# Rows of a multiple of 128 bytes for the moving operands, weights an odd multiple of 64 bytes from them

## The chip, the cores and the metric

The kernel runs on one core of a Trainium2 chip. The metric is the time of one execution on the device, in microseconds (us); lower is better. Three runs of the kernel before give a median of 2256.5 us (2256.18 to 2257.68).

## What is computed

One decoder layer on 1040 tokens (16 learned meta tokens ahead of 1024) of width 1024, in float32: a half-step feed-forward network, a mixing block with two groups of heads, a second feed-forward network, and a last norm. Cut to what matters:

```python
n = rms_norm(h, ffn1_norm)
h = h + 0.5 * ((silu(n @ w_gate) * (n @ w_up)) @ w_down)      # D_FF = 2816
n = rms_norm(h, mix_norm)
proj = n @ w_in                                               # 3 * 512 + 1696 columns
sb_out = stick_breaking_attention(q, k, v)                    # 8 heads of 64
rw_out = rwkv7_time_mix(proj[..., 1536:], ...)                # 8 heads of 64
h = h + concatenate([sb_out, rw_out]) @ w_out
n = rms_norm(h, ffn2_norm)
h = h + 0.5 * ((silu(n @ w_gate2) * (n @ w_up2)) @ w_down2)
return rms_norm(h, final_norm)[:, 16:]
```

The products with w_gate, w_up, w_down, w_in and w_out are the dense products of the title.

## The kernel before, in words

Activations are kept transposed: 128 of the 1024 features on the partitions, tokens along the row. The tokens are worked in two groups, A of 528 (16 + 512) and B of 512. A dense product takes a weight tile of 128 x 128 as the stationary operand and up to 512 tokens of an activation tile as the moving one, and sums eight such steps (or as many as the part of w_down has) in a PSUM bank.

To keep float32's precision with a faster type, every operand is split into a high and a low part of type float32r, and each step is three matmuls (mm3, line 680): high weights by high activations, high by low, low by high. ScalarE (ACT) makes the high part by a copy, VectorE (DVE) or GpSimd (POOL) the low part by a subtraction (split, line 498). Weights come from DRAM into the ring wr of two raw tiles, are split into the rings wh and wl of two tiles each (wsplit, line 526), and are used once or twice.

The moving operands are these tiles. `n` (ntiles, line 854): four tiles of 4 rows, high and low, each row NA = 528 floats. `n2B`, the same for group B of the second network, rows of 512. `ah` and `al` (act_tiles, line 947): the outcome of silu(gate) * up, one row of NA floats, in rings of four. A row is read in chunks: 512 columns at once, or 256 and 272 (256 and 256) where the network begins or ends.

Two stages work in another way. For a part of ffn1's group A and of ffn2's group B, pairs of gate or up tiles are multiplied by a scheme of Strassen's kind with seven products in place of eight ("quads": class Fast, line 466; pair, 577; sums, 1109; quad, 1143). `sums` makes four combinations of activations, the tiles t1 to t4 (4 rows of w = 264 or 256 floats); `pair` makes five combinations of weights, split into the rings qh and ql of seven tiles each; `cc` is a ring of seven tiles in which outcomes are added up. A weight tile there has rows of `qrow` = 128 + w % 128 floats, that is 136 where w is 264, and the offset of rows grows alike on both sides.

The order of the work is made when the program is built: Clock and Task (lines 168 to 460) run the stages as coroutines against costs of each instruction, and give a ring's next buffer out when its last reader is done. A coroutine says what it needs (`need`, `room`), with the ring's length beside it. The engines then follow the order written, with semaphores. TensorE works its queue in order; the waits that it meets are those on DVE, ACT or a ring of PSUM banks.

Tiles of a pool lie one behind the other, in steps of 32 bytes, and pools one behind the other; so a tile's size sets the place of all tiles behind it. Tiles that matter for places: `sl` (a gate's or up's outcome, 512 floats, two buffers), `nacc`, `nsq` and `ny` (272 floats) of the norms, `ones` (128 used floats of 152), and `f` of the attention.

The root of the norm (norm_root, line 819) is a row of reciprocal roots; norm_end (line 833) puts it into a tile `ny` of a ring of one, scales h by it and splits the outcome into `n`.

Of the kernel before, what the change touches and what calls it, by code (L numbers as in the profile page):

```python
# [7 lines left out]
F32 = mybir.dt.float32  # L8
# [8 lines left out]
P = 128  # L17
# [22 lines left out]
        dict(raw=1, qs=4, kh=4, vs=2, sg=8, f=2, at=4, z=2, t=2, o=1)]  # L40
WOUT = ((0, 1, 2, 3, 4, 5, 6, 7, 2, 3, 4, 5), (0, 1, 2, 3, 4, 5, 6, 7))
QF = dict(ffn1=6, ffn2=4)
QROW = P + 8
AHEAD = 0.1
IDLE = 0.45
BACKLOG = 3.0
# [419 lines left out]
class Fast:  # L466
# [2 lines left out]

    def __init__(self, pools, w):  # L470
        self.p, self.tp, self.q = pools
        self.w, self.nq, self.nc, self.ns, self.k = w, 7, 7, 4, 0
        self.qrow = P + w % P
        self.t = {i: [self.tp.tile([P, 4, w], F32R, name="t%d%s" % (i, c)) for c in "hl"] for i in (1, 2, 3, 4)}


class Ker:
# [40 lines left out]
    def wraw(self, src, nk, nm, ring=None):  # L518
# [4 lines left out]
        self.clock.ahead = False  # L523
        return raw

    def wsplit(self, raw, nk, nm, pool):
        self.clock.ahead = True
        self.nsplit = getattr(self, "nsplit", 0) + 1
        hi = pool.tile([P, nk, nm], F32R, tag="wh", bufs=2, name="whi")
        lo = pool.tile([P, nk, nm], F32R, tag="wl", bufs=2, name="wlo")  # L530

        self.split(hi, lo, raw, self.nc.gpsimd if self.nsplit < 3 else None)
        self.clock.ahead = False
        return hi, lo
# [42 lines left out]
    def pair(self, raws, out):  # L577


        nc, p = self.nc, self.fast.q  # L580
        nb, qrow = self.fast.nq, self.fast.qrow
        a1, a2 = raws
        lo4, hi4 = slice(0, 4), slice(4, 8)

        def part(src=None):

            for tag in ("qh", "ql"):
                yield self.need(bank=(p, tag, nb))
            if src:
                yield self.need(bank=(p, "qs", 3))  # L590
            self.clock.ahead = True
            t = [p.tile([P, 4 * QROW], F32R, tag=tag, bufs=nb, name=tag) for tag in ("qh", "ql")]
            t = [x[:, 0:4 * qrow].rearrange("p (k m) -> p k m", m=qrow)[:, :, 0:P] for x in t]
            self.hold(t)
            if src:
                x, y, op, eng = src
                raw = p.tile([P, 4 * P + 16], F32, tag="qs", bufs=3, name="qs")[:, 0:4 * P].rearrange("p (k m) -> p k m", m=P)
                self.hold((raw,))
                eng.tensor_tensor(out=raw, in0=x, in1=y, op=op)
                self.clock.ahead = False  # L600
                return t, raw
            return t

        def halves(t, raw):
            self.clock.ahead = True
            self.split(t[0], t[1], raw)
            self.clock.ahead = False
            self.drop((raw,))
            out.append((t, t))
        for tag in ("wh", "wl"):  # L610
            yield self.need(bank=(self.wp, tag, 2))
        self.clock.ahead = True
        w = [self.wp.tile([P, KT, P], F32R, tag="w" + c, bufs=2, name=n) for c, n in (("h", "whi"), ("l", "wlo"))]
        self.hold(w)
        self.clock.ahead = False
        s1 = yield from part((a2[:, lo4], a2[:, hi4], ALU.add, nc.gpsimd))
        self.clock.ahead = True
        self.split(w[0], w[1], a1)
        out.append(([w[0][:, lo4], w[1][:, lo4]], ()))
        out.append(([w[0][:, hi4], w[1][:, hi4]], w))  # L620
        self.clock.ahead = False
        s2 = yield from part((s1[1], a1[:, lo4], ALU.subtract, nc.vector))
        halves(*s1)
        a22 = yield from part()
        self.split(a22[0], a22[1], a2[:, hi4])
        self.clock.ahead = False
        s4 = yield from part((a1[:, hi4], s2[1], ALU.subtract, nc.vector))
        halves(*s2)
        out.append((a22, a22))
        s3 = yield from part((a1[:, lo4], a2[:, lo4], ALU.subtract, nc.gpsimd))  # L630
        halves(*s4)
        halves(*s3)
# [71 lines left out]
    def consts(self, cp):  # L704
        nc = self.nc
        self.ident = cp.tile([P, P], F32, name="ident")
        make_identity(self.tc.nc, self.ident)
        self.ones = cp.tile([P, P + 24], F32, name="ones")[:, 0:P]
        nc.gpsimd.memset(self.ones, 1.0)

    def consts2(self, cp, xp, psp):
# [121 lines left out]
    def norm_end(self, s, h, cols, gain, n, bank, now=True):  # L833

        nc, tp = self.nc, self.fp
        w = cols.stop - cols.start
        ys = []

        def new():
            ys.append(tp.tile([P, 272], F32, tag="ny", bufs=1, name="ny"))  # L840
            self.hold(ys)
            return ys[0][:, :w]
        yield from self.norm_root(s, w, new, bank, ("ny", 1))
        y = ys[0][:, :w]
        for k in range(KT):
            yield from self.room(tp, ("sl", 2) if k % 2 else ("nsq", 4))
            with self.urgent() if now else nullcontext():
                f = tp.tile([P, 512], F32, tag="sl", bufs=2, name="nf")[:, :w] if k % 2 else tp.tile([P, 272], F32, tag="nsq", bufs=4, name="nf")[:, :w]
                nc.vector.scalar_tensor_tensor(f, h[:, k, cols], self.v(gain, k), y, ALU.mult, ALU.mult)
                self.split(n[0][k][:, cols], n[1][k][:, cols], f, nc.gpsimd if k % 2 else None)  # L850
        self.drop(ys)
        yield self.need(*[x for k in range(KT) for x in (n[0][k][:, cols], n[1][k][:, cols])])

    def ntiles(self):

        half = [[self.hp.tile([P, 4, NA], F32R, tag="n%s%d" % (c, q), name="n%s%d" % (c, q)) for q in range(2)] for c in "hl"]
        return [[half[c][k // 4][:, k % 4, :] for k in range(KT)] for c in range(2)] + half

    def block(self, xts, m, xp, bank, out, hot=None):
# [37 lines left out]
    def ffn(self, nm, h, n, chunks, edge, bank, first=None, hook=None, wx=False, poll=None, resid=None, done=None, wy=False, fast=False, once=False):  # L897
# [32 lines left out]
        def gate(w, c0, c1):  # L930
            pg = yield from mm(*w, "pg", c0, c1)
            with self.urgent():
                sl = tp.tile([P, 512], F32, tag="sl", bufs=2, name="sl")[:, :c1 - c0]
                nc.scalar.activation(sl, pg, AF.Silu if fast else AF.Sigmoid)
                if not fast:

                    nc.vector.tensor_tensor(out=sl, in0=pg, in1=sl, op=ALU.mult)
            self.hold((sl,))
            return sl

        def up(w, sl, act, c0, c1, last):
            pu = yield from mm(*w, "pu", c0, c1)
            with self.urgent():
                nc.vector.tensor_tensor(out=sl, in0=pu, in1=sl, op=ALU.mult)
                self.split(act[0][:, c0:c1], act[1][:, c0:c1], sl, None if last else nc.gpsimd)
        gu = lambda ap, f, keep=False: self.wget(ap[:, :, f * P:f * P + P], KT, P, keep)
        act_tiles = lambda c=None: [c.q.tile([P, 2 * c.w], F32R, tag="q" + t, bufs=2, name=t) if c else
                                    tp.tile([P, NA], F32R, tag=t, bufs=4, name=t) for t in ("ah", "al")]

        def gates(f):  # L950
            if poll:
# [902 lines left out]
    def attn_z(self, pr, g, bufs, ops, out):  # L1854
# [6 lines left out]
        for i in (2 * pr, 2 * pr + 1):  # L1861
# [18 lines left out]
            for sg in sgs:  # L1880
                nc.gpsimd.affine_select(out=sg[:, S - P:S], in_=sg[:, S - P:S], pattern=[[-1, P]],
                                        compare_op=ALU.is_gt, fill=0.0, base=0, channel_multiplier=1)
                yield from self.room(ap, ("f", bufs["f"]))
                f = ap.tile([P, n], F32, tag="f", bufs=bufs["f"], name="f")
                nc.scalar.activation(f[:, :S], sg[:, :S], AF.Copy, scale=-1.0, bias=1.0)
                V.tensor_tensor_scan(f[:, S - 1::-1], f[:, S - 1::-1], f[:, S - 1::-1], 1.0, ALU.mult, ALU.bypass)
                nc.gpsimd.tensor_tensor(out=sg[:, 0:S - 1], in0=sg[:, 0:S - 1], in1=f[:, 1:S], op=ALU.mult)
# [646 lines left out]
```

## Time and profile before

| | |
|---|---|
| median of 3 runs | 2256.5 us |
| the profiled execution | 2258.75 us |
| its span (first to last instruction) | 2257.0 us |
| mean granted clock of TensorE | 0.997 |
| TensorE (PE), matmuls | 2227.9 us busy, 16409 instructions |
| weight loads (PEld) | 1972.8 us |
| VectorE (DVE) | 1550.8 us |
| ScalarE (ACT) | 1097.6 us |
| GpSimd (POOL) | 561.7 us |

Busy times of engines overlap. A matmul that overlaps the next is counted once in the busy time, while its "mean ns of one" is its own length from start to modelled end, so that for matmuls in a row the spacing from start to start is shorter than that length. Every operation is recorded by one helper, so all lines are L105 and groups are told apart by tiles: `pg<-nh,whi` is a matmul into the PSUM tile pg with nh moving and whi as weights. pg and pu are the products with w_gate and w_up, pd those with w_down and w_in, pwo that with w_out, po the attention's with v. In the chain of waits, neighbours on one engine with the same output are merged into one piece with its length and count.

### The profile page before, as it was taken

Reading aid. Unit: us, or ns where it says so; the run is one execution under the profiler, and the core shown is the slowest. Engines: PE = TensorE matmul, PEld = TensorE weight load, DVE = VectorE, ACT = ScalarE, POOL = GpSimd, SP = SyncE. Lnnn points to the kernel's source line nnn. Section 1 sums busy time; section 2 is a strip of 40 time slices with the busy share of each in tenths; the row PEclk is TensorE's granted clock in tenths of the full one; section 3 lists DMA queues with packets and bytes.
Section 4 is the critical chain, followed back from the end, with each engine's and each line's share of the span. In section 5 each row is a group of like instructions: output and inputs, shape, how many; then the busy total and the mean of one; then the engine's idle time right before and its main releaser. Section 6 shows DMA issues by size and latency. Waiting matters only on the chain.

```text
span 2257.0 us, 41723 instructions
## 1 busy us (share of the span) xinstructions
PE 2227.9 (99%) x16409; PEld 1972.8 (87%) x16409; DVE 1550.8 (69%) x2633; ACT 1097.6 (49%) x2176; POOL 561.7 (25%) x722
## 2 busy tenths in 40 slices
PE   9999999999999999999999999999999999999998
PEld 8999999999878888778878987887878899899998
DVE  5887776575666655566576887556777656897774
ACT  5444444544444534555435564445656436455444
POOL 1221111013142231442012324314443101221110
PEclk9999999999999999999999999999999999999999
DMA  5543232545633232332556534333222433333332
GB/s 167 175 119 103 81 108 78 164 129 137 204 104 102 71 102 88 108 92 71 153 146 189 167 101 117 86 93 118 82 79 61 131 117 121 113 103 104 112 88 81
DMA packets 408731, 257.62 MB, mean 114 GB/s; under 512 B 45005, under 2 KB 392357, under 8 KB 408534
## 3 DMA queue, kind: packets, MB, share of 16 engines
q1 hardware_dynamic: 408534, 254.95, 39.0%
q8 instruction: 129, 2.11, 0.4%
q14 instruction: 68, 0.56, 0.1%
HBM read 220.90 MB, written 33.99 MB: 113 GB/s over the span
## 4 chain that ended last, share of the span: by engine, by line
PE 92%; DVE 4%; ACT 1%; DMA 1%; issue 1%; POOL 0%; SPq 0%; DVEq 0%; ACTq 0%; POOLq 0%
PE pd L105 35%; PE pu L105 21%; PE pg L105 20%; PE pwo L105 4%; PE px L105 3%; PE po L105 2%; PE pz L105 2%; PE pat L105 2%; DVE wlo L105 1%; PE pG L105 1%; DVE tt L105 0%; PE psw L105 0%; ACT whi L105 0%; PE pp L105 0%; PE pss L105 0%
## 5 line engine op out<-in xcount | busy, mean ns | idle before, releaser
L105 ACT ACTIVATE whi<-wraw 128x1024 fp32r<-128x1024 f32 x314 | 330.5, 1053 | 339.0 <-PE pd L105 209.7
L105 DVE TENSOR_TENSOR wlo<-wraw,whi 128x1024 fp32r<-128x1024 f32 (+1 forms) x312 | 402.7, 1291 | 98.4 <-ACT whi L105 92.2
L105 PE MATMUL pd<-ah,whi 128*128 128x512 f32 (+2 forms) x944 | 326.0, 345 | 4.4 <-DVE h L105 3.6
L105 PE MATMUL pd<-ah,wlo 128*128 128x512 f32 (+2 forms) x944 | 319.3, 338 | 1.2 <-DVE wlo L105 1.2
L105 PE MATMUL pd<-al,whi 128*128 128x512 f32 (+2 forms) x944 | 319.0, 338 | 0.3
L105 PE MATMUL pd<-nh,whi 128*128 128x256 f32 (+7 forms) x648 | 210.9, 326 | 0.0
L105 PE MATMUL pu<-nh,whi 128*128 128x512 f32 (+3 forms) x576 | 206.4, 358 | 0.0
L105 PE MATMUL pd<-nl,whi 128*128 128x256 f32 (+7 forms) x648 | 205.4, 317 | 0.0
L105 PE MATMUL pd<-nh,wlo 128*128 128x256 f32 (+7 forms) x648 | 205.0, 316 | 0.0
L105 PEld LDWEIGHTS pd<-ah,whi 128*128 128x128 f32 x944 | 177.6, 188 | 27.3 <-DVE h L105 4.8
L105 PE MATMUL pg<-nh,whi 128*128 128x512 f32 (+3 forms) x536 | 197.6, 369 | 0.9 <-ACT nh L105 0.7
L105 PE MATMUL pu<-nl,whi 128*128 128x512 f32 (+3 forms) x576 | 197.9, 344 | 0.0
L105 PE MATMUL pu<-nh,wlo 128*128 128x512 f32 (+3 forms) x576 | 197.8, 343 | 0.0
L105 PEld LDWEIGHTS pd<-ah,wlo 128*128 128x128 f32 x944 | 177.8, 188 | 22.5 <-DVE wlo L105 2.1
L105 PEld LDWEIGHTS pd<-al,whi 128*128 128x128 f32 x944 | 177.8, 188 | 18.6 <-DVE al L105 1.5
L105 PE MATMUL pg<-nl,whi 128*128 128x512 f32 (+3 forms) x536 | 188.7, 352 | 0.9 <-DVE nl L105 0.9
L105 PE MATMUL pg<-nh,wlo 128*128 128x512 f32 (+3 forms) x536 | 188.4, 351 | 0.0
L105 POOL TENSOR_TENSOR qs<-wraw 128x512 f32<-128x512 f32 x64 | 96.5, 1511 | 369.1 <-DVE ql L105 122.3
L105 DVE SCALAR_TENSOR_TENSOR h<-pd,h 128x256 f32<-128x256 f32 (+1 forms) x200 | 107.5, 541 | 75.9 <-PE pd L105 74.8
L105 POOL TENSOR_TENSOR al<-sl,ah 128x512 fp32r<-128x512 f32 (+2 forms) x45 | 72.8, 1617 | 320.0 <-ACT ah L105 316.8
L105 PEld LDWEIGHTS pd<-nh,whi 128*128 128x128 f32 (+2 forms) x648 | 120.8, 186 | 12.4 <-issue 3.1
L105 PEld LDWEIGHTS pd<-nh,wlo 128*128 128x128 f32 (+2 forms) x648 | 120.9, 187 | 8.5
(395 smaller groups left out, 5640.2 us busy)
## 6 DMA issues: line engine op xcount, KB each, us to landing
wraw<-in_ffn_w_gate_dram SPq DMA_DIRECT2D x90, 512.0 KB
wraw<-in_ffn_w_up_dram SPq DMA_DIRECT2D x90, 512.0 KB
wraw<-in_ffn_w_down_dram SPq DMA_DIRECT2D x88, 512.0 KB
wraw<-in_w_in_dram SPq DMA_DIRECT2D x54, 512.0 KB
wraw<-in_w_out_dram SPq DMA_DIRECT2D x20, 512.0 KB
s<-rkvd SPq DMA_DIRECT2D x18, 256.0 KB
raw<-qkvd SPq DMA_DIRECT2D x16, 264.0 KB
raw<-qkvd SPq DMA_DIRECT2D x16, 256.0 KB
```

The source lines that it names most:

```text
L105: self._c.trace(self._n, op, lambda: f(*a, **k), out, [x for x in args if isinstance(x, bass.AP)], k)
```

## The change

Places and ring lengths, and nothing else: no instruction is added or left out.

- The tiles n, ah, al (and the quads' acts) get rows of ROW = 544 floats (2176 bytes, 17 times 128) in place of 528. Of t1 to t4, rows are rounded up to a multiple of 32 floats (288 for 264).
- Split weights go through `wtiles`: 1024 floats and 32 more, begun 16 floats (64 bytes) on in the pool wx.
- The quads' weights get rows of 128 floats, in tiles of 544, begun 16 floats on, and 24 floats on for the one that meets a moving tile begun 264 floats into a row. The rings qh, ql and cc go from seven tiles to six. `qs` loses its 16 floats of margin.
- The norm's root takes its tile from the ring nacc of two, and the ring ny goes away.
- `sl` gets 8 floats more, and `f` in the second attention too; `ones` is written in another way with the same size.

```diff
-QROW = P + 8
+LINE = 16
+NQ, NCC = 6, 6
+ROW = 544
...
-        self.w, self.nq, self.nc, self.ns, self.k = w, 7, 7, 4, 0
-        self.qrow = P + w % P
-        self.t = {i: [self.tp.tile([P, 4, w], F32R, name="t%d%s" % (i, c)) for c in "hl"] for i in (1, 2, 3, 4)}
+        self.w, self.nq, self.nc, self.ns, self.k = w, NQ, NCC, 4, 0
+        r = -(-w // (2 * LINE)) * 2 * LINE
+        self.t = {i: [self.tp.tile([P, 4, r], F32R, name="t%d%s" % (i, c))[:, :, 0:w] for c in "hl"] for i in (1, 2, 3, 4)}
...
+    def wtiles(self, nk, nm, pool):
+
+        o = LINE * (pool is self.wx)
+        t = [pool.tile([P, 8 * P + 2 * LINE], F32R, tag=t, bufs=2, name=n) for t, n in (("wh", "whi"), ("wl", "wlo"))]
+        return [x[:, o:o + nk * nm].rearrange("p (k c) -> p k c", c=nm) for x in t]
...
-        hi = pool.tile([P, nk, nm], F32R, tag="wh", bufs=2, name="whi")
-        lo = pool.tile([P, nk, nm], F32R, tag="wl", bufs=2, name="wlo")
+        hi, lo = self.wtiles(nk, nm, pool)
...
-        def part(src=None):
+        def part(src=None, o=0):
...
-            t = [p.tile([P, 4 * QROW], F32R, tag=tag, bufs=nb, name=tag) for tag in ("qh", "ql")]
-            t = [x[:, 0:4 * qrow].rearrange("p (k m) -> p k m", m=qrow)[:, :, 0:P] for x in t]
+            t = [p.tile([P, 4 * P + 2 * LINE], F32R, tag=tag, bufs=nb, name=tag) for tag in ("qh", "ql")]
+            t = [x[:, LINE + o:LINE + o + 4 * P].rearrange("p (k m) -> p k m", m=P) for x in t]
...
-        w = [self.wp.tile([P, KT, P], F32R, tag="w" + c, bufs=2, name=n) for c, n in (("h", "whi"), ("l", "wlo"))]
+        w = self.wtiles(KT, P, self.wp)
...
-        s4 = yield from part((a1[:, hi4], s2[1], ALU.subtract, nc.vector))
+        s4 = yield from part((a1[:, hi4], s2[1], ALU.subtract, nc.vector), self.fast.w % (2 * LINE))
...
-            ys.append(tp.tile([P, 272], F32, tag="ny", bufs=1, name="ny"))
+            ys.append(tp.tile([P, 272], F32, tag="nacc", bufs=2, name="ny"))
...
-        yield from self.norm_root(s, w, new, bank, ("ny", 1))
+        yield from self.norm_root(s, w, new, bank, ("nacc", 2))
...
-        half = [[self.hp.tile([P, 4, NA], F32R, tag="n%s%d" % (c, q), name="n%s%d" % (c, q)) for q in range(2)] for c in "hl"]
+        half = [[self.hp.tile([P, 4, ROW], F32R, tag="n%s%d" % (c, q), name="n%s%d" % (c, q)) for q in range(2)] for c in "hl"]
...
-                sl = tp.tile([P, 512], F32, tag="sl", bufs=2, name="sl")[:, :c1 - c0]
+                sl = tp.tile([P, 512 + LINE // 2], F32, tag="sl", bufs=2, name="sl")[:, :c1 - c0]
...
-        act_tiles = lambda c=None: [c.q.tile([P, 2 * c.w], F32R, tag="q" + t, bufs=2, name=t) if c else
-                                    tp.tile([P, NA], F32R, tag=t, bufs=4, name=t) for t in ("ah", "al")]
+        act_tiles = lambda c=None: [c.q.tile([P, ROW], F32R, tag="q" + t, bufs=2, name=t) if c else
+                                    tp.tile([P, ROW], F32R, tag=t, bufs=4, name=t) for t in ("ah", "al")]
...
-                f = ap.tile([P, n], F32, tag="f", bufs=bufs["f"], name="f")
+                f = ap.tile([P, n + LINE // 2 * g], F32, tag="f", bufs=bufs["f"], name="f")
```

More of the change, by code (lines that the diff above doesn't have):

```diff
@@ L580, in pair @@
         nc, p = self.nc, self.fast.q
-        nb, qrow = self.fast.nq, self.fast.qrow
+        nb = self.fast.nq
         a1, a2 = raws
         lo4, hi4 = slice(0, 4), slice(4, 8)
-        def part(src=None):
+        def part(src=None, o=0):
             for tag in ("qh", "ql"):
@@ L596, in part @@
                 x, y, op, eng = src
-                raw = p.tile([P, 4 * P + 16], F32, tag="qs", bufs=3, name="qs")[:, 0:4 * P].rearrange("p (k m) -> p k m", m=P)
+                raw = p.tile([P, 4, P], F32, tag="qs", bufs=3, name="qs")
                 self.hold((raw,))
@@ L707, in consts @@
         make_identity(self.tc.nc, self.ident)
-        self.ones = cp.tile([P, P + 24], F32, name="ones")[:, 0:P]
+        self.ones = cp.tile([P, P + 3 * LINE // 2], F32, name="ones")[:, 0:P]
         nc.gpsimd.memset(self.ones, 1.0)
```

## The prediction

> **What bounds the kernel now.** I read the page first, for the engine that sets the end, then the waits of TensorE, then the groups by shape, and last the chain of waits piece by piece, because only there the spacing of one matmul to the next can be seen.
>
> ```profile
> span 2257.0 us, 41723 instructions
> PE 2227.9 (99%) x16409; PEld 1972.8 (87%) x16409; DVE 1550.8 (69%) x2633; ACT 1097.6 (49%) x2176; POOL 561.7 (25%) x722
> ...
> PEclk9999999999999999999999999999999999999999
> ...
> PE 92%; DVE 4%; ACT 1%; DMA 1%; issue 1%; POOL 0%; SPq 0%; DVEq 0%; ACTq 0%; POOLq 0%
> ...
> PE pd L105 <- DVE h L105: 3.6, 4, 1.7
> ...
> PE pg L105 <- DVE ql L105: 0.9, 1, 0.9
> ```
>
> TensorE is busy for 2227.9 of 2257.0 us, its granted clock is at nine tenths or more in every slice, and its waits for any one partner come to 3.6 us at most (the columns of the last two lines: us in total, times, longest). So the time can only fall if the matmuls themselves stand closer together, and every nanosecond of their spacing counts in full. The profiled execution took 2258.75 us, 1.75 us more than its span and 2.25 us more than the median of 2256.5 us; I make the sum against 2258.75 and take 2.25 off at the end.
>
> The next rows are the timeline, one matmul with the weight load (PEld) of the next one beside it.
>
> ```profile
> 1001.03 0.40 PE L105 MATMUL pu<-nh,wlo 128*128 128x512 f32 x1
> 1001.03 0.19 PEld L105 LDWEIGHTS pu<-nh,whi 128*128 128x128 f32 x1
> 1001.27 0.39 PE L105 MATMUL pu<-nh,whi 128*128 128x512 f32 x1
> ```
>
> The load of the next weights starts with the matmul before it, so TensorE reads two places of SBUF at once: the moving operand of this matmul and the weights of the next. The change alters only where these two lie to each other. Does that matter? The chain of waits holds a clean test, eight moving rows of 256 columns from the tile n2B, whose rows are 2048 bytes (16 times 128).
>
> ```profile
> 1896.85 2.38 PE pu L105 x21
> ...
> 1900.86 2.88 PE pg L105 x24
> ```
>
> The columns are start and length in us, the engine, the tile written and the number of matmuls. Per matmul this is 113.3 ns in the first piece, whose weights come from the pool w, and 120.0 ns in the second, whose weights come from the pool wx. Moving operand, shape and work are the same; the pools' starts differ by an odd multiple of 64 bytes, which follows from the sizes of the tiles laid out before them. So the place matters, by 6.7 ns of 120, and the weights of w stand at the good distance, those of wx at the bad one. But the good distance isn't enough:
>
> ```profile
> 1802.55 44.52 PE pwo L105 x378
> ...
> 1937.71 5.59 PE pu L105 x24
> 1943.30 5.60 PE pg L105 x24
> ...
> 1966.55 9.53 PE pg L105 x84
> ...
> 2087.65 9.80 PE pu L105 x84
> ...
> 2193.67 9.65 PE pg L105 x84
> ```
>
> All of these have rows in multiples of 128 bytes and weights at the good distance. The 378 of w_out, 256 wide, take 117.8 ns each; the quads of ffn2 (16 such pieces of 84, of which the first, the longest and the last are shown) 113.5 to 116.7 ns, on average 114.2; and the products 512 wide 232.9 and 233.3 ns. So 256 columns have two steady spacings at the good distance, near 113.4 and near 118, and a run can stay in either. For comparison, pieces on rows of 528 floats (2112 bytes, 16.5 times 128, so that the distance alternates from row to row):
>
> ```profile
> 135.99 10.16 PE pg L105 x84
> ...
> 342.99 10.19 PE pg L105 x84
> ...
> 593.02 2.84 PE pg L105 x24
> ...
> 737.22 5.56 PE pg L105 x24
> ```
>
> 256 columns take 118.3 ns, 512 columns 231.7 ns, and the quads of ffn1 (264 columns, 15 pieces of 84 from the first to the last shown) 121.0 to 121.3 ns.
>
> **The change part by part.** Counts come from the groups by shape. Each row stands for three of equal count (high by high, low by high, high by low). The "mean ns of one" holds a modelled drain of about 163 ns: 395 against the spacing of 231.7, and 276 against 113.5 in the quads.
>
> ```profile
> L105 PE MATMUL pd<-al,whi 128*128 128x512 f32 x464 | 182.7, 394 | 0.1
> ...
> L105 PE MATMUL pg<-nl,whi 128*128 128x512 f32 x328 | 129.6, 395 | 0.0
> ...
> L105 PE MATMUL pu<-nl,whi 128*128 128x512 f32 x312 | 123.2, 395 | 0.0
> ...
> L105 PE MATMUL pd<-al,whi 128*128 128x256 f32 x304 | 85.4, 281 | 0.1
> ...
> L105 PE MATMUL pd<-nl,whi 128*128 128x256 f32 x240 | 67.5, 281 | 0.0
> ...
> L105 PE MATMUL pd<-nl,whi 128*128 128x512 f32 x168 | 66.5, 396 | 0.0
> ...
> L105 PE MATMUL pd<-nl,whi 128*128 128x272 f32 x192 | 56.0, 292 | 0.0
> ...
> L105 PE MATMUL pd<-al,whi 128*128 128x272 f32 x176 | 50.9, 289 | 0.1
> ...
> L105 PE MATMUL pu<-nl,whi 128*128 128x256 f32 x144 | 40.4, 281 | 0.0
> ...
> L105 PE MATMUL pwo<-nl,whi 128*128 128x256 f32 x128 | 36.8, 288 | 0.0
> ...
> L105 PE MATMUL po<-ath,vs 128*128 128x256 f32 x128 | 35.4, 308 | 0.0
> ...
> L105 PE MATMUL pg<-nl,whi 128*128 128x256 f32 x96 | 27.0, 281 | 0.6 <-DVE nl L105 0.6
> ...
> L105 PE MATMUL pu<-nl,whi 128*128 128x272 f32 x64 | 18.5, 289 | 0.0
> ...
> L105 PE MATMUL pg<-nl,whi 128*128 128x272 f32 x48 | 13.9, 291 | 0.3 <-DVE nl L105 0.3
> ...
> L105 PE MATMUL pg<-n2Bh,qh 128*128 128x256 f32 x36 | 9.9, 276 | 0.0
> ```
>
> *256 columns, rows of 528 floats to 544.* 304+240+144+128+96 = 912, times 3 are 2736 matmuls at 281 - 163 = 118 ns, which is the 118.3 of the chain. Ends: 113.4 (the clean pieces), a gain of 4.9 ns, and 117.8 (w_out), a gain of 0.5. I take the mean of the 256-wide rows that have the new layout today, (1344 x 114.2 + 378 x 117.8) / 1722 = 115.0, so 3.3 ns less: 2736 x 3.3 = 9.0 us, between 1.4 and 13.4.
>
> *272 columns.* 192+176+64+48 = 480, times 3 are 1440, at 126 to 129 ns; I use 127. No row shows them in the new layout. Scaled from 113.4 by the columns the clean spacing would be 120.5, a gain of 6.5 ns or 9.4 us; at the other end nothing. Two thirds of the gap, as at 256, would be 4.3 ns; as it's another width I take half of that, 2.2 ns: 3.2 us.
>
> *264 columns, the quads of ffn1.* 15 x 84 = 1260 at 121.1. Their weights' rows already grow with the moving rows (QROW), so that two of three matmuls stand at the good distance; since every third load goes one row on; the change makes it three of three, with rows of 1152 and 512 bytes. Scaled, the clean spacing is 117.0, a gain of 4.1 ns or 5.2 us, the other end nothing. A third of it, 1.4 ns: 1.7 us.
>
> *512 columns.* 464+328+312+168 = 1272, times 3 are 3816, at 231.7. The nearest rows, the two pieces at 232.9 and 233.3, say 1.4 ns more, which is 5.3 us lost; twice 113.4 would be 226.8, 18.7 us gained. The two pieces have rows of 2048 bytes, all at one place of a 256-byte period; rows of 2176 bytes step by 128 in it, as the split weights of the ffn2 quads do today from buffer to buffer (544 floats each), and the quads are the fast ones. Between a measured small loss and that, I take no change.
>
> *Weights of wx (16 floats on), of attention, the norm's ring.* The wx weights cure the four products at 120.0 ns and the like: a few pieces of 24 like the one at 1900.86, each 24 x 6.7 ns = 0.16 us at best, left at nothing. The eight floats more of f in the second attention shift what lies behind it by 64 bytes, for `po` alone: 2 x 128 matmuls by 6.7 ns, 1.7 us at most either way, left at nothing. The norm's root loses its own buffer and takes one of the accumulators' ring of two; when it asks, the oldest of the two has been summed up already (norm_sums runs just before in the same task), so nothing is late; if that cover failed, the ACT copy of the root would wait, and behind it on ACT the splits of weights. The larger tiles add no instruction, no byte of a DMA, and no element to any engine's work. The Clock's costs don't know of places, so the order stays, but for the rings.
>
> *Rings of seven to six (qh, ql, cc).* A split into the ring can start when the product six parts back is done, not seven: one product of 12 matmuls later, 9.53 / 7 = 1.36 us. What hides it is the lead of the splits over TensorE. Bounds: nothing, and 1.36 us in each of 31 quad pieces, 42 us. The only wait of TensorE on these tiles is the 0.9 us above, in 31 quads; I take nothing.
>
> Sum: 9.0 + 3.2 + 1.7 + 0 = 13.9 us. 2258.75 - 13.9 = 2244.85, less 2.25 for the median: 2242.6 us.
>
> The Trainium skill, page "TensorE: Matmul & The Clock Gate", section "Back-to-back issue gap", gives an isolated warm gap of N/2.4 + 2.5 ns, 109.2 for 256 and 215.8 for 512 columns; by that floor the two widths alone would have 24.9 + 60.7 us to give (an estimate from that page). The trace doesn't reach it in any piece shown here, 113.3 being the lowest.
>
> **The rivals.** *Clean at every width.* If the distance is what keeps runs from 113.4, all go there: 13.4 + 9.4 + 5.2 + 18.7 = 46.7 us, median 2209.8. For it speaks the 6.7 ns between two pools; against it w_out, 378 in a row in the good layout and never clean, and the 512-wide pieces.
>
> *Nothing that can be measured.* Today's spacing on mixed rows is 118.3 and the w_out pieces have 117.8. If long runs settle in that state, 1.4 us are gained at 256 and nothing elsewhere: median 2255.1. For it speaks that w_out is the longest undisturbed run of its kind; against it the 16 quads. The Trainium skill, page "SBUF — State Buffer", section "Who interferes with whom", would also have no change: it calls TensorE's two read ports, moving operand and weights, independent. The pieces at 113.3 and 120.0 ns contradict that rule here, so it adds little to this case.
>
> *Slower by the rings.* The place is the quads, where DVE, ACT and POOL make five split pairs per product group. If the lead is under 1.36 us in most quads, each repeats the wait that one has now: 31 x 0.9 = 27.9 us lost against 13.9 gained, 14 us slower, median 2270.5. The waits speak against it, with one in 31. It decides from a lead of 1.36 us down.
>
> *The change doesn't do what it says*, one base being off by 64 bytes. Then the distance is the bad one in every row instead of every second, 120.0 for 118.3: 2736 x 1.7 = 4.7 us slower, median 2261.2. The sizes speak against it: a weight tile is 4224 bytes (33 times 128), two sl are 4160 (32.5 times), which sets the activations 64 bytes off the weights, and the norm's lost buffer, 1088 (8.5 times), gives the 64 bytes back to h and n.
>
> **How the numbers follow.** Chances: the forecast 0.64, clean 0.13, nothing 0.13, rings 0.07, not as said 0.03. No change to be told by a measurement is within 0.2%, 4.5 us. Of the forecast about 0.05 falls within that, so faster is 0.59 + 0.13 = 0.72, same 0.05 + 0.13 = 0.18, slower 0.07 + 0.03 = 0.10. The forecast's own range: at the low end every width clean but 512, and that half-way, 13.4 + 9.4 + 5.2 + 9.3 = 37 us, 2219; at the high end the gain at 256 of 1.4 us, 2255. The range of 2217 to 2256 leaves out the clean case and the rings, 2 in 10.
>
> **What would show it.** In the chain of waits of the changed kernel, 256-wide pieces outside the quads should come to 2.72 to 2.84 us per 24, quads of ffn1 to under 10.1 us per 84, 512-wide pieces of 24 stay between 5.5 and 5.6. The mean ns of `pd<-nl,whi` 128x256 should fall from 281 to about 278, that of 128x512 stay near 395. If 512-wide groups fall to 390, the clean case is right; if `pg<-DVE ql` grows beyond a few us in the waits, the rings. I'd be wrong in the reason if the time falls while the 256-wide groups keep 281.

## The result, and the profile after

The kernel after takes 2246.5 us (median of 6 runs, 2244.75 to 2247.88) against 2257.1 us before in the same comparison: a ratio of 0.9952, with a 95% interval from 0.9939 to 0.9965. That is 10.6 us less, where the prediction had 13.9 us. The profiled execution took 2247.88 us.

From the page of the kernel after, and from the waits of TensorE (us in total, times, longest):

```profile
span 2246.0 us, 41718 instructions
PE 2218.6 (99%) x16409; PEld 1967.9 (88%) x16409; DVE 1547.6 (69%) x2633; ACT 1096.6 (49%) x2176; POOL 574.1 (26%) x722
...
PEclk9999999999999999999999999999999999999999
```

```profile
PE pp L107 <- issue: 2.7, 1, 2.7
...
PE pd L107 <- DVE h L107: 2.0, 3, 0.8
```

The number of matmuls and the clock are the same; TensorE's busy time is 9.3 us shorter. The wait for `ql` is gone, and no wait has grown by as much as a microsecond (the largest step is `pp`, 1.9 to 2.7 us), so the gain lies in the spacing of matmuls. Where, the chain of waits tells (start, length, tile, count):

```profile
134.11 10.19 PE pg L107 x84
...
340.89 10.21 PE pg L107 x84
...
588.38 2.81 PE pg L107 x24
...
638.48 5.52 PE pg L107 x24
...
1794.18 43.48 PE pwo L107 x378
...
1892.02 2.72 PE pg L107 x24
...
1928.27 5.60 PE pu L107 x24
...
1957.03 9.69 PE pg L107 x84
```

Read against the pieces of before: the quads of ffn1 stay (121.0 to 121.3 ns each before, 121.3 to 121.5 now); 256 columns on the wide rows go from 118.3 to 117.1 ns; 512 columns from 231.7 to 230.0 (5.56 to 5.52 us per 24); w_out's 378 from 117.8 to a mean of 115.0, which the experiment on what ran before takes apart; the product at 1892, with weights from the second weight pool, from 120.0 to 113.3; n2B at 512 columns (1928) stays at 233.3. The groups by shape say the same, the mean length of one in the last number before the bar:

```profile
L107 PE MATMUL pd<-al,whi 128*128 128x512 f32 x464 | 181.7, 392 | 0.4 <-DVE al L107 0.3
...
L107 PE MATMUL pd<-al,whi 128*128 128x256 f32 x304 | 85.3, 281 | 0.2
...
L107 PE MATMUL pd<-nl,whi 128*128 128x256 f32 x240 | 67.1, 280 | 0.0
...
L107 PE MATMUL pd<-nl,whi 128*128 128x272 f32 x192 | 55.4, 288 | 0.0
```

The 512 wide groups fell from 394 to 392, the 272 wide from 292 to 288, and the 256 wide hardly moved (281 and 281 before). For the sums I took every time from one start to the next inside a product, waits left out, from the traces of all layer kernels. Means in ns:

| moving rows | before | after | wrong distance | control | rows of 256's multiples | same, 512 wide at 64 | high and low together | all at 64, 192, 64 |
|---|---|---|---|---|---|---|---|---|
| 256 columns of n, ah, al | 118.0 | 117.3 | 118.6 | 117.3 | 116.6 | 116.7 | 117.8 | 117.7 |
| 256 columns of n2B | 116.8 | 115.3 | 119.2 | 115.1 | 116.5 | 116.8 | 114.3 | 114.2 |
| 256 columns, quads of ffn2 | 113.9 | 114.2 | 119.0 | 114.0 | 115.0 | 114.2 | 113.4 | 113.5 |
| 264 columns, quads of ffn1 | 121.2 | 121.4 | 121.9 | 121.6 | 121.5 | 121.5 | 121.5 | 121.5 |
| 272 columns | 125.9 | 125.1 | 125.6 | 125.2 | 123.7 | 123.7 | 124.7 | 124.7 |
| 512 columns of n, ah, al | 232.0 | 230.2 | 231.9 | 230.2 | 228.9 | 233.0 | 231.3 | 231.3 |

Before to after, by the counts of the groups: 512 columns 3816 x 1.75 = 6.7 us; 256 columns 2736 x 0.7 = 1.9; n2B 1128 x 1.5 = 1.7; 272 columns 1440 x 0.8 = 1.2; the attention's `po` 256 x 2.4 = 0.6 (118.0 to 115.6); the quads' products with split sums as weights give back 0.2 in ffn1 (900 of them) and 0.3 in ffn2 (1020). That is 11.6 us; the spans differ by 11.0. So the total came out near the forecast, but more than half of it from the width for which the forecast was nothing.

### The profile page after: what moved, and what is told of

It is laid out like the page before. It is cut to its first block, busy times and chain, and to the rows that moved or that the text cites. A ratio compares the mean times of both kernels' runs of the same rounds, so it can differ in the third digit from the quotient of the medians.

```text
span 2246.0 us, 41718 instructions
## 1 busy us (share of the span) xinstructions
PE 2218.6 (99%) x16409; PEld 1967.9 (88%) x16409; DVE 1547.6 (69%) x2633; ACT 1096.6 (49%) x2176; POOL 574.1 (26%) x722
## 4 chain that ended last, share of the span: by engine, by line
PE 91%; DVE 3%; issue 2%; ACT 2%; DMA 1%; SPq 1%; POOL 0%; DVEq 0%; ACTq 0%; POOLq 0%
PE pd L107 33%; PE pu L107 21%; PE pg L107 21%; PE pwo L107 3%; PE px L107 3%; PE po L107 2%; PE pz L107 2%; PE pat L107 2%; DVE wlo L107 1%; SPq L107 1%; PE pG L107 1%; ACT whi L107 1%; PE psw L107 0%; PE pp L107 0%; DVE nl L107 0%
## 5 line engine op out<-in xcount | busy, mean ns | idle before, releaser
L107 POOL TENSOR_TENSOR qs<-wraw 128x512 f32<-128x512 f32 x64 | 106.1, 1660 | 358.1 <-DVE ql L107 133.5
```

Source lines behind the costliest of these rows:

```text
L107: self._c.trace(self._n, op, lambda: f(*a, **k), out, [x for x in args if isinstance(x, bass.AP)], k)
```

## The experiments

My theory going in: a matmul is stretched when the next weights stand at an even multiple of 64 bytes from the moving row, and an odd multiple is good. The rivals: place doesn't matter and the time came from elsewhere; traffic of other engines makes the second spacing (118) at the good distance; the place in a longer period than 128 bytes matters; what ran before matters; rings hide a loss.

**TensorE alone, place by place.** A kernel of nothing but matmuls, in stages; the weights' and rows' places are cut out of two large tiles, hi and lo weights 4224 bytes apart. This was meant to be the layer's layout, but isn't: in the pool the two high tiles lie ahead of the two low ones, so the layer's kernel after has high and low weights of one product 2 x 4224 = 8448 bytes apart, which is 33 times 256. The stage's low weights stand 128 bytes off that place modulo 256, and its distances go 64, 192, 64 where the layer's go 64, 64, 64 or 192, 192, 192 on one row.

```python
def stage(name, w, pitch, off, base, reps=5):
    o, b = (off + base) // 4, base // 4
    wh = [wt[:, o + k * P:o + k * P + P] for k in range(8)]
    wl = [wt[:, 1056 + o + k * P:1056 + o + k * P + P] for k in range(8)]
    xh = [big[:, b + k * pitch:b + k * pitch + w] for k in range(8)]
    xl = [big[:, b + (8 + k) * pitch:b + (8 + k) * pitch + w] for k in range(8)]
    for _ in range(reps):                 # hh, hl, lh for k = 0 to 7, as mm3 does
        ...
STAGES = dict(a=(256, 544, 0, 0), c=(256, 544, 64, 0), f=(256, 512, 64, 0), h=(256, 512, 192, 0), i=(256, 528, 64, 0), ...
```

> This kernel leaves the whole layer out: it only multiplies, TensorE alone, 24 stages of 120 matmuls each (and once more in reverse order), every stage with its own width, step from row to row and distance from the moving rows to the weights; the output is a copy of the input's first rows. If the place of moving rows and weights to each other sets the spacing (my theory), 256 columns take 119 to 120 ns at 0 and 128 bytes, and 113 to 118 ns at 64 and 192; 512 columns 233 ns at 0 and 227 to 231 at 64; 272 columns 127 at 0 and 121 to 125 at 64. If the two read ports are independent (rival), all stages of one width take the same within 0.5 ns. If it is the change of place from row to row that costs (second rival), the stages on rows of 528 floats are the slow ones and 0 is as fast as 64.

The timeline has the first matmul of each stage (the first column is its start; pc and rc are the stage c in the two orders); the distance of two starts, over 120, is the spacing.

```profile
54.40 0.28 PE L60 MATMUL pc<-big,wt 128*128 128x256 f32 x1
68.28 0.28 PE L60 MATMUL pd<-big,wt 128*128 128x256 f32 x1
...
96.96 0.28 PE L60 MATMUL pf<-big,wt 128*128 128x256 f32 x1
110.60 0.28 PE L60 MATMUL pg<-big,wt 128*128 128x256 f32 x1
124.79 0.28 PE L60 MATMUL ph<-big,wt 128*128 128x256 f32 x1
138.39 0.28 PE L60 MATMUL pi<-big,wt 128*128 128x256 f32 x1
152.70 0.39 PE L60 MATMUL pj<-big,wt 128*128 128x512 f32 x1
180.56 0.39 PE L60 MATMUL pk<-big,wt 128*128 128x512 f32 x1
208.23 0.39 PE L60 MATMUL pl<-big,wt 128*128 128x512 f32 x1
...
764.59 0.28 PE L60 MATMUL rh<-big,wt 128*128 128x256 f32 x1
778.86 0.28 PE L60 MATMUL rg<-big,wt 128*128 128x256 f32 x1
```

256 columns: on rows of 544 at 64 bytes (pc) 13.88 / 120 = 115.7 ns, on rows of 512 at 64 (pf) 113.7, on rows of 528 (pi) 119.2. Place matters with TensorE alone, so the independent ports are out. The second rival, that only the change from row to row costs, falls too: on rows of 512 the stage at 0 takes 119.1 against 113.7 at 64. But the stage h is 113.3 in one order (ph) and 118.9 in the other (rh): what ran before counts as well. At 512 columns, rows of 544, 0 against 64 bytes is 232.2 against 230.6 (pj, pk); at 272 it's 125.5 against 126.7 or 125.5, so nothing there; 264 columns have 122.1 against 121.1. On rows of 544, 256 columns at 0 take 117.8, where 119 to 120 was expected, and 118.5 and 119.9 at 32 and 96 bytes. A parity worth about 5 ns appears only where all rows lie in steps of 2048 bytes. A base 96 bytes on changed nothing beyond 0.3 ns.

**With the other engines busy.** The same stages, with this beside them:

```diff
+        for i in range(760):
...
+            nc.scalar.activation(hi, src, AF.Copy)
+            nc.vector.tensor_tensor(out=lo, in0=src, in1=hi.bitcast(F32), op=ALU.subtract)
+            if i % 4 == 0:
...
+                nc.sync.dma_start(out=wr, in_=x[0:P, :])
```

> The same matmuls as in the run with TensorE alone, with a copy on ScalarE, a subtraction on VectorE and a load of 512 KB beside them all the time (the layer is left out here too). It tells why the good distance has two spacings in the layer, near 113.4 and near 118. If traffic of the other engines makes the second one, 256 columns at 64 bytes stay at 113.4 with TensorE alone and go to 116 to 118 here. If the matmuls make it by themselves, both runs show the same within 0.5 ns, stage by stage.

```profile
55.86 0.28 PE L60 MATMUL pc<-big,wt 128*128 128x256 f32 x1
69.75 0.28 PE L60 MATMUL pd<-big,wt 128*128 128x256 f32 x1
```

115.7 ns again, and all 48 stages agree with the quiet run within 0.02 ns; ScalarE and VectorE worked through all of them, the loads through the first of the two orders. So TensorE shows the two spacings by itself, and traffic of these three kinds is out; GpSimd, and reads of PSUM, weren't tried beside it.

**The wrong distance in the layer.**

```diff
-        o = LINE * (pool is self.wx)
+        o = LINE * (pool is not self.wx)
...
-            t = [x[:, LINE + o:LINE + o + 4 * P].rearrange("p (k m) -> p k m", m=P) for x in t]
+            t = [x[:, o:o + 4 * P].rearrange("p (k m) -> p k m", m=P) for x in t]
```

> The kernel after with all split weights 64 bytes off: every row at the bad distance, no mixed rows. By my theory all widths go to the spacing of the bad distance. From the means after (256 columns 117.3 on the 2736, 115.3 on the 1104 of n2B, 114.2 in the 1344 of the quads; 264 columns 121.4; 272 columns 125.1; 512 columns 230.2) to 119.7, 123.6, 127 and 233.3: 6.6 + 4.9 + 7.4 + 2.8 + 2.7 + 11.8 = 36 us, so 2283 us, 26 us slower than before. If the ports are independent: 2246 us, like after. If only mixed rows cost: 2246 us too.

2264.2 us, a ratio to before of 1.0037 (1.0022 to 1.0051): 8 us slower than before and 18 us slower than after. The place is the cause of the change's gain, but I had asked for 36 us.

```profile
641.93 5.57 PE pg L107 x24
...
1964.85 10.00 PE pg L107 x84
```

The quads of ffn2 went near the 119.7 ns expected (119.0), n2B too (119.2). The wide rows didn't: 118.6 where 119.7 stood, 231.9 where 233.3 stood. On rows of 544 the even multiple isn't as bad, as the odd one isn't as good. The sums by counts are good to some us only: here they give 21 us over the kernel after, the medians 18, the spans of the profiled executions 15.

**Rings of six.**

```diff
-        self.w, self.nq, self.nc, self.ns, self.k = w, 7, 7, 4, 0
+        self.w, self.nq, self.nc, self.ns, self.k = w, 6, 6, 4, 0
```

> The kernel before with the quads' rings of six in place of seven and no other change: the places of all rows stay. My step says 0 us: 2257 us. If the shorter rings cost and the places gained more than the total shows: 2260 to 2285 us, with waits of TensorE for ql or cc in the quads.

2255.45 against 2256.13 us, a ratio of 0.9997 (0.9988 to 1.0006): nothing, as the step had it.

**A finer period.** Rows in steps of 2048 bytes, hi and lo weights 5120 bytes apart, so that one stage has one place modulo 512.

```diff
...
-            wl = [wt[:, 1056 + o + k * P:1056 + o + k * P + P] for k in range(8)]
+            wl = [wt[:, 1280 + o + k * P:1280 + o + k * P + P] for k in range(8)]
```

> Only multiplies, like the two runs of stages before (the layer is left out). Here every row lies in steps of 2048 bytes and the high and low weights 5120 bytes apart, so that in a stage the distance to the next weights is the same modulo 512 bytes for every matmul; the stages are 0, 64, ... 448 bytes for 256, 512 and 272 columns, each in two orders. If only the parity of 64 bytes decides (my theory), the four stages at 64, 192, 320 and 448 are alike within 0.5 ns and quicker than the four others by 3 ns or more, at each width. If a finer place decides (rival), some of the odd ones are at 113.4 (226.7, 120.4) and others at 118 (233, 127), the same in both orders. If what came before decides (second rival), one and the same stage differs between the two orders, as 256 columns at 192 bytes did with 113.34 and 118.92 ns.

```profile
70.14 0.28 PE L60 MATMUL pd<-big,wt 128*128 128x256 f32 x1
84.27 0.28 PE L60 MATMUL pe<-big,wt 128*128 128x256 f32 x1
...
141.19 0.40 PE L60 MATMUL pi<-big,wt 128*128 128x512 f32 x1
168.45 0.40 PE L60 MATMUL pj<-big,wt 128*128 128x512 f32 x1
196.45 0.39 PE L60 MATMUL pk<-big,wt 128*128 128x512 f32 x1
...
880.90 0.28 PE L60 MATMUL rd<-big,wt 128*128 128x256 f32 x1
894.50 0.28 PE L60 MATMUL rc<-big,wt 128*128 128x256 f32 x1
```

512 columns take 27.26 / 120 = 227.2 ns at 0 (pi) and 233.3 at 64 (pj): the other way round than at 256 columns. Every place equals the one 256 bytes on, within 0.4 ns where history plays no part, so the period is 256 bytes. In ns:

| from the row to the next weights, modulo 256 | 0 | 64 | 128 | 192 |
|---|---|---|---|---|
| 256 columns | 120.0 | 117.8 or 113.3 | 118.6 | 117.8 or 113.3 |
| 512 columns | 226.9 | 233.3 | 232.4 | 228.9 |
| 272 columns | 125.3 | 123.3 | 126.7 | 126.7 |

The stage d is 117.8 in one order (pd) and 113.3 in the other (rd). My theory of the parity falls here; both rivals, the finer place and what ran before, stand.

**What ran before.** One line of matmuls; a stage of 96 entered in seven ways from 512 columns:

```python
PAT = dict(a=(64, 64, 64), b=(192, 192, 192), c=(64, 192, 64), d=(192, 64, 192))   # after hh, hl, lh
ENT = dict(a=(0, 0), b=(1, 0), c=(2, 0), d=(3, 0), e=(1, 128), f=(2, 128), g=(3, 128))
```

> Only multiplies (the layer is left out). 256 columns on rows in steps of 2048 bytes, in four patterns of the distance to the next weights modulo 256 bytes: always 64, always 192, 64-192-64, 192-64-192. Each pattern is entered in seven ways, after 24 matmuls of 512 columns at 0 with none to three matmuls of 256 columns at 0 or at 128 between, and then runs for 96 matmuls. If what comes before decides between 113.3 and 117.8 ns (my theory, from one stage that gave 113.34 and 118.92 in two orders), the two constant patterns show both values, by the entry, and stay in them; if alternation frees a run, 64-192-64 shows 113.3 to 113.6 for every entry. If the place alone decides (rival), each pattern has one value for all seven entries.

Rows of a tile's instructions give the lengths of one (least, median, most, in ns), and the first and last start; paa is pattern a entered with no matmul between, pab with one.

```profile
L56 PE MATMUL paa<-big,wt x96: 280/281/281, 43.0 to 54.2; 128*128 128x256 f32 x96
...
L56 PE MATMUL pab<-big,wt x96: 276/276/384, 60.0 to 70.9; 128*128 128x256 f32 x96
...
L56 PE MATMUL pca<-big,wt x96: 276/276/282, 279.6 to 290.4; 128*128 128x256 f32 x96
```

A single matmul ahead decides: 281 ns long (117.8 from start to start) or 276 (113.3), and the run stays there for all 96. Always 64 was clean after five of seven entries, always 192 after one, 192-64-192 after four (the others 118.9), and 64-192-64 after all seven.

The layer shows both spacings inside one run. These are w_out's matmuls with low activations, first of the kernel before, then of the kernel after in two windows of the run of 378:

```profile
L105 PE MATMUL pwo<-n2Bl,whi x126: 281/281/282, 1802.5 to 1846.7; 128*128 128x256 f32 x126
```

```profile
L107 PE MATMUL pwo<-n2Bl,whi x48: 279/280/281, 1794.1 to 1810.8; 128*128 128x256 f32 x48
...
L107 PE MATMUL pwo<-n2Bl,whi x75: 276/276/276, 1811.8 to 1836.9; 128*128 128x256 f32 x75
```

The kernel after starts at the slow spacing, 117.8 ns, and after six products of 24 goes over to 113.3, without a gap, and keeps it to the end. So 115.0 is no spacing but a mean of the two. The distance was an odd multiple of 64 bytes before as well: w_out's 378 x 2.8 = 1.1 us, of the 1.7 us gained on n2B, are this second spacing and not a cure of the distance. What made it go over at the seventh product was not found.

**Rows of 256's multiples in the layer, its counterpart, and a control.** Rows of 576 floats, hi and lo weights in one tile 4096 bytes apart, the weights' place chosen by the width that will use them. That needs room, so two rings got shorter; the control has only that.

```diff
-        dict(raw=1, qs=4, kh=4, vs=2, sg=8, f=2, at=4, z=2, t=2, o=1)]
+        dict(raw=1, qs=4, kh=4, vs=2, sg=7, f=2, at=4, z=2, t=2, o=1)]
...
-NQ, NCC = 6, 6
-ROW = 544
+O512, O256, OX = 16, 32, 16
+NQ, NCC = 6, 5
+ROW = 576
...
+        t = pool.tile([P, 16 * P + 4 * LINE], F32R, tag="wh", bufs=2, name="whl")
+        return [t[:, i:i + nk * nm].rearrange("p (k c) -> p k c", c=nm) for i in (o, o + 8 * P)]
```

> The kernel after with rows of 576 floats (a multiple of 256 bytes), high and low weights 4096 bytes apart, and the distance of the weights chosen by the width of their use: 0 modulo 256 for most of the 512 wide products, 64 for 256 and 272 columns (192 for n2B); to make room, cc is a ring of five and one ring of the second attention a ring of seven. If the place modulo 256 bytes and the width decide, as the stages alone showed (512 columns 226.9 at 0; 272 columns 123.3 at 64; 256 columns 113.3 or 117.8), 512 columns go from 230.2 to about 227.2 on some 3500 matmuls, 10.5 us, 272 columns from 125.1 to 123.5 on 1270, 2.0 us, and 256 columns lie between 4.2 us worse (all at 117.8) and 13 us better: 2238 us, between 2221 and 2239. If the parity of 64 bytes is what matters, the 512 wide products are now at the wrong parity and go to 233.3: 3500 x 3.1 = 10.9 us slower than after, 2257 us.

The counterpart has `O512, O256, OX = 32, 32, 16`:

> The kernel of rows in multiples of 256 bytes with one number changed: the weights of the 512 wide products stand at 64 modulo 256 bytes as all others do. It holds the change's own rule (weights an odd multiple of 64 bytes from the rows) in every row. By the place modulo 256 the 512 wide go to 233.3, so 3500 x 6.1 = 21 us slower than at 0. By the parity of 64 bytes it is the better one, by 21 us.

The control has the lines of `NCC` and `sg` alone:

> The kernel after with only what the kernel with rows of 256 bytes' multiples gave up for room: cc a ring of five, one ring of the second attention seven. No place of the dense products changes its distance. 2246.5 us like after, within 0.2%, if those rings are as slack as the quads' others; over 2251 us if they cost, and then that cost is to be added to what the places gain.

2296.0 us (ratio to before 1.0176, 1.016 to 1.0191), 2307.3 (1.0226, 1.0209 to 1.0244) and, the control, 2299.0 (1.0189, 1.0173 to 1.0204). The control was expected at 2246.5: shortening `cc` from six to five and `sg` from eight to seven costs 53 us, which made the 2238 I expected of the first impossible. Which of the two rings it is wasn't tried, and the order of the work came out another way with them (16417 matmuls in place of 16409). The control's waits, and its windows with the granted clock as the last number but two:

```profile
PE pwo L107 <- ACT n2Bh L107: 12.1, 2, 10.0
PE pg L107 <- ACT t1h L107: 10.9, 3, 5.0
PE pwo L107 <- DVE wlo L107: 8.2, 6, 5.2
```

```profile
1800.00:1850.00 50.00, 39.83 (x234) 32.80 (x232) 29.88 (x40) 19.04 (x36) 6.44 (x5) 0.94 0.23 68
...
2000.00:2050.00 50.00, 41.81 (x293) 39.44 (x294) 42.80 (x68) 25.02 (x49) 13.83 (x12) 0.82 0.22 64
```

31 us of waits in those three rows, and in the same stretch a granted clock down to 0.82 in windows of 50 us (1.00 in the same windows of the kernel after).

The first two differ by one number and 11.4 us, in favour of 0 bytes for 512 columns. The same group in the first and in the second:

```profile
L108 PE MATMUL pg<-nl,whl 128*128 128x512 f32 x328 | 128.2, 391 | 0.0
```

```profile
L108 PE MATMUL pg<-nl,whl 128*128 128x512 f32 x328 | 129.5, 395 | 0.0
```

228.9 against 233.0 on average, so 3816 x 4.1 = 15.6 us, of which 0.8 us go back in the quads of ffn2 (1020 x 0.8). 227.2 was expected of the first; 272 columns came to 123.7 as expected (123.5), 256 columns to 116.6. The odd multiple of 64 bytes, held in every row, is the bad place for 512 columns here. Against the control, the places gain 3.1 us, which the intervals don't separate.

**High and low rows together.** To fix the place modulo 256 without more room, hi and lo of one row lie side by side (4352 bytes), and the products get 0, 0, 0 (512 wide) or 64, 192, 64.

```diff
+O512, O256, ON, OX = (16, 16), (32, 0), (0, 0), 0
...
-        half = [[self.hp.tile([P, 4, ROW], F32R, tag="n%s%d" % (c, q), name="n%s%d" % (c, q)) for q in range(2)] for c in "hl"]
+        both = [self.hp.tile([P, 4, 2 * ROW], F32R, tag="n%d" % q, name="n%d" % q) for q in range(2)]
+        half = [[t[:, :, c * ROW:c * ROW + ROW] for t in both] for c in range(2)]
```

> The kernel after with its ring lengths, laid out so that the place modulo 256 bytes stays fixed without more room: each row of n and of the acts holds its high and its low half of 544 floats side by side (4352 bytes, 17 times 256), and high and low split weights share a tile. From the row to the next weights it is 0, 0, 0 modulo 256 bytes in the 512 wide products, and 64, 192, 64 in those of 256 and 272 columns, the pattern that was clean after every entry. If place modulo 256 and width decide: 512 columns from 230.2 to about 227.2 on 3700 matmuls, 11 us; 256 columns on the rows of n and the acts from 117.3 to 113.7 on 2736, 9.8 us; on n2B from 115.3 to 113.7 on 1104, 1.8 us; 272 columns from 125.1 to 124.4, 1 us: 23 us in all, 2223 us, between 2214 and 2236. If the parity of 64 bytes were the rule, the 512 wide products would be at the wrong parity, 233.3, and lose 11 us: 2247 us. If a shorter or shared ring costs as in the control, waits of TensorE for ACT or DVE show it.

The second kernel has (32, 0) as the first pair:

> The kernel with the high and low rows side by side and one number pair changed: the 512 wide products stand at 64, 192, 64 like the narrower ones, so that every product holds to the change's own rule (weights an odd multiple of 64 bytes from rows of a multiple of 128). From the stages alone, 512 columns at 64, 192, 64 take 231.8 against 226.9 at 0: 3700 x 4.7 = 17 us slower than at 0. If the change's rule were right at this width, it would be no slower, and up to 20 us faster.

2250.6 us for the first (0.9965 to before, 0.9953 to 0.9978) and 2251.5 for the second (0.9973, 0.9961 to 0.9985): neither is better than the kernel after, and the place of the 512 wide products made no difference (231.3 ns in both), where 17 us were expected. In the first:

```profile
639.44 5.55 PE pg L108 x24
...
1794.96 42.85 PE pwo L108 x378
```

512 columns stand at 231.3 where about 227 was expected, 256 columns on n and the acts at 117.8. On n2B the same distances do work: 42.85 / 378 = 113.4. The difference is that n2B has hi and lo rows at one place modulo 256, while here each low row lies 128 bytes off its high one. So the distance from row to weights isn't all; the moving rows' places among themselves must count.

**Moving rows' steps.** Stages with a fixed distance r to the next weights and a fixed step s from one moving row to the next:

```python
x = (i % 16) * 512 + m(i) // 4                               # m(i) = i * s % 256
o = (i % 8) * P + (m(i - 1) + r(i - 1)) % 256 // 4
mm(ps, lhsT=wt[:, o:o + P], rhs=big[:, x:x + w], start=i == 0, stop=i == 23)
```

> Only multiplies (the layer is left out). Stages of 72 matmuls of 256, 512 and 272 columns; in each the next weights stand at a fixed distance r (0, 64, 128, 192 modulo 256 bytes) from the moving row, and each moving row stands s (0, 64, 128, 192) on from the one before; at the end the two arrangements of the last two layer kernels, with low rows 128 bytes off the high ones and with both at one place. If r alone decides (what I built the high and low rows side by side on), s makes no difference: 512 columns at r = 0 take 226.9 for each s, and the arrangement with low rows 128 off takes 113.3 and 226.9 ns. If the moving rows' own places count as well (my theory now, from 231.2 instead of 227 in that kernel and 113.6 on n2B, whose high and low rows stand at one place): at s = 128, r = 0 512 columns take 231 or more, the arrangement 128 off takes 117 to 119 and 231, the one without 113.3 and 226.9. 272 columns are 17 times 64 bytes: if what counts is that the stream of moving rows runs on through the 256 bytes without a jump, the clean 120.4 appears for them at s = 64 and at no r with s = 0.

The arrangement with low rows 128 bytes off (pga 256, pgb 512 columns), and the same with both at one place (pgd, pge):

```profile
L54 PE MATMUL pga<-big,wt x72: 277/281/283, 584.2 to 592.5; 128*128 128x256 f32 x72
...
L54 PE MATMUL pgb<-big,wt x72: 387/393/399, 592.7 to 609.1; 128*128 128x512 f32 x72
...
L54 PE MATMUL pgd<-big,wt x72: 276/276/279, 618.3 to 626.3; 128*128 128x256 f32 x72
...
L54 PE MATMUL pge<-big,wt x72: 388/389/397, 626.4 to 642.5; 128*128 128x512 f32 x72
```

From start to start, the first third of a stage left out: 117.8 and 231.2 ns against 113.3 and 226.7. The layer had 117.8 and 231.3. At a step of 128 bytes 256 columns take 116.7 for every r, clean nowhere; at a step of 0 the table above comes back, save that in one of the two orders 512 columns at 128 and 192 are at 233.3 and 272 columns at 0 at 126.7; 512 columns at r = 0 take 226.7, 231.7, 230.0 and 233.0 for steps of 0, 64, 128 and 192. So both places count. The further thought, that the stream of rows must run on without a jump, falls: 272 columns took 125.6 to 126.1 at s = 64, and were at 120.4 in no stage.

## Why the prediction was right, and where it was not

**The bound** held: the time fell by what the matmuls moved together, 11.6 us by spacings against 11.0 in the span.

**The premise** failed in part: "the weights of w stand at the good distance, those of wx at the bad one". For those pieces it's true (the cure of wx brought 120.0 to 113.3), but I read a parity of 64 bytes out of n2B's rows and carried it to rows of another step and to other widths. The stages show a period of 256 bytes, another best place for each width, a part for the step between moving rows, and a part for what ran before. Measured alone, the arrangements come out near their spacings in the layer, save for 256 columns. Only the last row repeats the layer's distances in full, and there all three widths agree within 0.2 ns; in the stages of the first three the low weights stand 128 bytes off the layer's place modulo 256:

| ns, TensorE alone / in the layer | 256 columns | 272 columns | 512 columns |
|---|---|---|---|
| rows of 528 (before) | 119.2 / 118.0 | 125.5 / 125.9 | 231.6 / 232.0 |
| rows of 544, odd (after) | 115.7 / 117.3 | 126.7 or 125.5 / 125.1 | 230.6 / 230.2 |
| rows of 544, even (wrong distance) | 117.8 / 118.6 | 125.5 / 125.6 | 232.2 / 231.9 |
| high and low together | 117.8 / 117.8 | 124.5 / 124.7 | 231.1 / 231.3 |

**256 columns**, predicted at 9.0 us: 1.9 came, near the low end of 1.4. The mean of "the 256-wide rows that have the new layout today" was mostly quads, whose rows don't step by 2176 bytes. Why the layer has 117.3 and the stage 115.7 wasn't tested. The stage's distances aren't the layer's, as said at the first experiment, which is the nearest reason; that products of other shapes break in is a guess.

**512 columns**, predicted at 0 between a loss of 5.3 and a gain of 18.7: 6.7 us gained. The two pieces of n2B at 233, my "nearest rows", have another step, and stayed at 233.3 in the kernel after too.

**272 columns**: 1.2 us for 3.2. **264 columns**: a loss of 0.2 for a gain of 1.7. **wx, w_out and po**, left at nothing: 1.7 us on n2B and 0.6 on `po`. Three pieces of 24 like the one at 1900.86 (0.5 us) could have been counted from that row; 1.1 us are w_out's run going over to its other spacing, which was luck.

**Rings**: 0, as measured alone. How far the slack goes this step doesn't say: the control cut `cc` once more, with one ring of the attention, and lost 53 us.

**The rivals.** "Clean at every width" fell: with TensorE alone the new layout isn't clean at any width. "Nothing that can be measured" fell by the interval. The rings' rival fell with rings of six; that the change doesn't do what it says fell with the wrong distance, 18 us slower.

**What would show it**: 256 wide pieces at 2.81 lie in the 2.72 to 2.84 named, 512 wide ones at 5.52 in 5.5 to 5.6, but the quads of ffn1 stayed over 10.1, and the 256 wide groups kept 281 and 280. By my own test the time fell and the reason for the largest term was wrong. The total was near by luck: 7.1 us too much at 256 columns, 6.7 us too little at 512.

## What to carry to other kernels

Where TensorE is the bound and the products run back to back, the places of moving rows and of the next weights are worth a few per cent of each matmul (113.3 to 120.0 ns for 256 columns alone), though this layer gained 0.5% from them: measure them with TensorE alone, in the very order and step of rows that the kernel has, for each width by itself, since a rule from one width and step didn't hold at others. Rows all at one place modulo 256 bytes, with weights at 0 for 512 columns and at 64, 192, 64 for 256 columns, were the only arrangements that were clean, at 226.7 and 113.3 ns with TensorE alone, after every entry tried; in the layer the first came to 228.9 on average. But room isn't free: one tile fewer in each of two rings cost 53 us, five times the gain. No kernel that was run is better than the one after.

## What the runs showed of the hardware

With TensorE alone and nothing changed but places, 256 columns took 113.3 to 120.0 ns, 512 columns 226.7 to 236.7. The Trainium skill, page "SBUF — State Buffer", section "Who interferes with whom", has TensorE's two read ports independent; on this chip, in this type, a measurement speaks against that. Traffic of ScalarE, VectorE and DMA beside it changed nothing (0.02 ns), which agrees with the same section.

A run of equal matmuls can stay in one of two spacings, 113.3 or 117.8 ns, for 96 in a row, by one matmul ahead of it; in the kernel after, w_out's run of 378 went from the second to the first midway. The lowest spacing of float32r in any stage was 113.3 ns for 256 and 226.7 for 512 columns. What in SBUF or TensorE makes a period of 256 bytes was not found.
